# A ready time moved back by one microsecond in the list schedule of the second mixer's unit matmuls

## The chip, the cores and the metric

The kernel runs on one core of one Trainium2 chip. The metric is the device time of one execution in microseconds, as the median of the runs of a kernel. The profile and its trace come from one further execution on the same core.

## The reference, cut to what matters

Two decoder layers on 256 tokens of width 2048, all in float32. The first layer mixes tokens with RWKV-7, the second with a chunked gated DeltaNet; behind each comes a gated MLP with a short convolution, and behind every part a layer norm. The change lies in the second mixer:

```python
def gated_deltanet(x, w_in, conv_w, a_log, dt_bias, norm_w, w_out):
    proj = x @ w_in
    qkv, z, b, a = jnp.split(proj, ...)
    qkv = silu(causal_dwconv(qkv, conv_w))
    q, k, v = ...                              # 16 key heads, 32 value heads of 128
    o = chunk_gated_delta_rule(q, k, v, g, beta)
    o = o * rsqrt(mean(o * o) + NORM_EPS) * norm_w * silu(z)
    return o.reshape(B, T, GDN_VALUE_DIM) @ w_out
```

The delta rule solves a unit lower triangular system in each chunk and head (`Tm = triangular_solve(A + eye, eye)`), and carries a state from one chunk to the next.

## The kernel before, in words

Products of float32 numbers are made from two parts of each operand, a rounded one (`whi`, `xhl`) and the rest (`wlo`), three matmuls for a product. The weights stream from memory: a tile `raw` is loaded, ScalarE casts it to `whi`, VectorE subtracts to get `wlo`, TensorE multiplies. These projections are the *main* stream. In the second mixer they are written (`gdn`, L1531) as eight rounds, u = 0 to 7; each round projects the q, k, v and z of four value heads (576 matmuls of 128x256 named `mm<-xhl,whi` and `mm<-xhl,wlo`). Behind the eighth round comes the output projection, whose matmuls are named `tm<-whi,ohl`.

After each round `gdn_unit` (L1645) records a *unit*, the delta rule of those four heads, as a side stream. A unit is one long chain that goes to and fro between the engines. The names that the text uses, in order of the chain: `vT` and `kqT` (transposes), `sq`, `ssq`, `rn`, `nk` (norms), `kk` (products of keys), `lt` and `at` (masked with decays `gr`), then the inverse (`inverse`, L917): `uc`, `z`, `spread`, the matmul `blocks`, fourteen small VectorE steps `t` and `v`, `vx`, the matmul `zp<-vx`, `n<-x,ld`, three matmul groups `y`, `zp<-y`, `xt`, `xb` (two of them), two groups `n<-xb`, six groups `y`; then for each of two chunks the solve (`u<-rhr,y`, `au`, `du`, `un`), `S`, `ks`, `qs`, `os`, `o`, `ms` and the transpose `oT`, whose result `og` the output projection reads.

Nothing is issued in the order in which it is written. Every operation is first recorded, and a list scheduler (`order`, L364) replays the whole program against estimated durations (`cost`) and hand-over times (`LAT`, `LAT_TO`) and writes out one order for each engine; each engine then runs its list in that order. All instructions carry line 556, the line that issues them, so names and not lines tell them apart. At most two units (`DEPTH_G = 2`) are open at a time. Some steps (`nc.two`, `nc.copy`) have a form for two engines, and the scheduler picks one: `spread`, `xb`, `uc<-uc` and `o<-o,os` on VectorE or GpSimd.

At each step the scheduler takes the operation with the smallest key. For a unit's matmul the key began with `s`, the later of the time at which TensorE is free and the time at which the operands are estimated to be there; a main matmul with the same time comes behind it. So a unit's matmul was put in front of the main ones at the very moment at which its operands were estimated to be ready.

Of the kernel before, what the change touches and what calls it, by code (L numbers as in the profile page):

```python
# [28 lines left out]
NU = 8  # L29
# [52 lines left out]
class Buf:  # L82


    def __init__(self, pool, shape, dtype, tag, bufs, name, real=None):
        self.pool, self.shape, self.dtype, self.name, self.real = pool, list(shape), dtype, name, real
        self.group = None if pool is None else pool.group(tag or name, bufs)
        self.tag = tag or name
        self.writers, self.readers, self.uses = [], [], 0
        self.pe = self.read = None  # L90
        self.end = 0.0
# [60 lines left out]
class View:  # L152
# [5 lines left out]
    def then(self, shape, dtype, *op):  # L158
        return View(self.buf, shape, dtype, self.ops + (op,))
# [72 lines left out]


class Op:
    __slots__ = ("lazy", "eng", "calls", "dur", "preds", "succ", "soft", "at", "bufs", "news", "stream", "idx", "npred", "ready",
                 "out", "fn", "alts", "least", "held", "evac", "table")


# [13 lines left out]
class Plan:  # L252
# [2 lines left out]


    def __init__(self, tc):
        self.lazy = 0.0
        self.tc, self.real = tc, tc.nc
        self.main = Stream(False, 0)  # L260
        self.streams, self.cur = [self.main], self.main
        self.last_pool = None
        self.tensor, self.vector, self.scalar, self.gpsimd, self.sync = (
            Engine(self, n) for n in ("tensor", "vector", "scalar", "gpsimd", "sync"))
# [9 lines left out]
    def op(self, eng, stream):  # L274
        o = Op()
        o.eng, o.calls, o.dur, o.preds, o.succ, o.soft, o.bufs, o.news = eng, [], 0.0, set(), [], [], set(), []
        o.stream, o.idx, o.ready, o.out, o.fn, o.alts = stream, len(stream.ops), 0.0, None, None, None
        o.npred, o.held, o.evac, o.lazy, o.table = 0, 0.0, [], self.lazy, None
        stream.ops.append(o)
        return o  # L280

# [18 lines left out]
    def two(self, out, x, y, op):  # L300
        self.either(*((e, "tensor_tensor", (out, x, y, op), {}) for e in ("vector", "gpsimd")))
# [62 lines left out]
    def order(self):  # L364
# [51 lines left out]
        while len(done) < total:  # L416
            best = None
            for e in engines:
                f = free[e]
                for o in cand[e]:  # L420
                    r = o.ready
                    ok = True
                    for b in o.news:
                        g = b.group
                        if g["free"] is None:
                            g["free"] = [0.0] * g["bufs"]
                        if (len(g["free"]) < len(o.news) or g["queue"][o.stream][0] not in o.news
                                or not self.spare(g, o, active)):
                            ok = False
                            break  # L430
                        r = max(r, g["free"][0])
                    if not ok:
                        continue
                    for b in o.evac:

                        if b.read is not None and b.read[0] != e:
                            r = max(r, b.read[1] + LAT[b.read[0]] + LAT_TO[e])
                    s = max(f, r)
                    if o.alts:
                        s += o.alts[e][3] - o.least  # L440
                    elif e == "scalar" and o.table not in (None, table):
                        s += TABLE
                    if e != "tensor":
                        key = (s, 0, o.ready - AGE_V * o.stream.age, o.idx)
                    else:
                        key = ((s, 0, o.ready - AGE * o.stream.age, o.idx) if o.stream.side
                               else (s + o.lazy, 1, o.idx, 0))
                    if best is None or key < best[0]:
                        best = (key, o, e, max(f, r))
# [5 lines left out]
            _, o, e, s = best  # L455
# [8 lines left out]
            dur = o.dur  # L464
# [3 lines left out]
            if e == "tensor":  # L468
                while (win + 1) * HAM <= s:
                    u = busy.get(win, 0.0) / HAM  # L470
# [133 lines left out]
KEEP = True  # L604
AGE, AGE_V, AGE_M = 1e5, 1e5, -9
HAM, HAM_ON, HAM_OFF = 4096 / 1.2, 0.7, 0.375
LAZY = 200.0

TABLE, TABLES = 1283.0, {AF.Tanh: 0, AF.Exp: 0, AF.Square: 0, AF.Silu: 1, AF.Ln: 2}
GROUP = 700.0  # L610
# [7 lines left out]
class Trunk:  # L618
# [468 lines left out]
    def rwkv(self):  # L1087
# [127 lines left out]
        wo = a["rw_w_o"]  # L1215
        nc.lazy = LAZY
        for c0, n in (0, 1024), (1024, 512):
# [313 lines left out]
    def gdn(self):  # L1531
        nc, a = self.nc, self.a
# [59 lines left out]
        def qkv(ps, b, nme, u, j, gblk):  # L1592
            d = st.setdefault(u, {})
            if nme == "q" and b == 0:
                d["KQ"] = self.ws.tile([P, 2, 2, 2, P], F32, tag="KQ", bufs=2, name="KQ")
            if nme == "v" and j == 0 and b == 0:
                d["v"] = self.ws.tile([P, 4, T], F32, tag="v_u", name="v_u")
            acc = self.conv(ps, gblk + b, 4, 64)
            if nme == "v":
                silu2(d["v"][:, 2 * j + b, :], acc)  # L1600
            else:
                silu2(d["KQ"][:, b, :, int(nme == "q"), :], acc)

        def zev(ps, b, u, j):
            d = st[u]
            if j == 0 and b == 0:
                d["z"] = self.ws.tile([P, 4, T], F32, tag="z_u", bufs=2, name="z_u")
            silu2(d["z"][:, 2 * j + b, :], ps)

        for u in range(NU):  # L1610
            self.proj_fm(w, u * 256, 256, xk, lambda ps, b, u=u: qkv(ps, b, "q", u, 0, 2 * u))
            if u == 0:
                self.proj_fm(w, 12288, 64, xk, gates)
            self.proj_fm(w, D + u * 256, 256, xk, lambda ps, b, u=u: qkv(ps, b, "k", u, 0, 16 + 2 * u))
            for j in range(2):
                self.proj_fm(w, 2 * D + u * 512 + j * 256, 256, xk,
                             lambda ps, b, u=u, j=j: qkv(ps, b, "v", u, j, 32 + 4 * u + 2 * j))
            for j in range(2):
                self.proj_fm(w, 4 * D + u * 512 + j * 256, 256, xk,
                             lambda ps, b, u=u, j=j: zev(ps, b, u, j))  # L1620
            with nc.unit(DEPTH_G):
                self.gdn_unit(u, st[u])

        self.ok = {}
        wo = a["gdn_w_out"]
# [249 lines left out]
```

## Time and profile before

| | |
|---|---|
| median of 3 runs | 3112.74 us (3106.1 to 3119.25) |
| the profiled execution | 3101.99 us, of which its span is 3100.3 us |
| TensorE busy | 2992.3 us, 97% of the span |
| VectorE busy | 2110.6 us, 68% |
| ScalarE busy | 1615.9 us, 52% |
| GpSimd busy | 651.7 us, 21% |
| granted TensorE clock, mean | 0.988 of 2.4 GHz |

Times in the trace count from the start of the span. The second mixer's projections run from 1420 us to 2158 us. The first unit's inverse begins at 1518 us, and a new unit follows every 90 us or so. TensorE is busy in nearly all of the span, so time is lost where it idles or where its clock is lowered.

### The profile page before, as it was taken

Reading aid. Unit: us, or ns where it says so; the run is one execution under the profiler, and the core shown is the slowest. Engines: PE = TensorE matmul, PEld = TensorE weight load, DVE = VectorE, ACT = ScalarE, POOL = GpSimd, SP = SyncE. Lnnn points to the kernel's source line nnn. Section 1 sums busy time; section 2 is a strip of 40 time slices with the busy share of each in tenths; the row PEclk is TensorE's granted clock in tenths of the full one; section 3 lists DMA queues with packets and bytes.
Section 4 is the critical chain, followed back from the end, with each engine's and each line's share of the span. In section 5 each row is a group of like instructions: output and inputs, shape, how many; then the busy total and the mean of one; then the engine's idle time right before and its main releaser. Section 6 shows DMA issues by size and latency. Waiting matters only on the chain.

```text
span 3100.3 us, 55990 instructions
## 1 busy us (share of the span) xinstructions
PE 2992.3 (97%) x22307; PEld 2797.3 (90%) x22307; DVE 2110.6 (68%) x3316; ACT 1615.9 (52%) x2713; POOL 651.7 (21%) x569
## 2 busy tenths in 40 slices
PE   8998999899999999998999999999999999999998
PEld 7998898779999998887999999999788999999886
DVE  7657878767666665447777777787767666666445
ACT  4437666445555554345556555555566555555333
POOL 3014344325010110003322112111233410101001
PEclk9999999999999999999999999999999999999999
DMA  6652213246666665665555554554465666666655
GB/s 198 206 165 89 74 58 97 68 132 199 189 184 188 186 184 190 193 192 155 169 151 150 143 144 137 143 155 131 152 192 182 201 188 185 188 186 186 192 189 187
DMA packets 436119, 503.64 MB, mean 162 GB/s; under 512 B 22769, under 2 KB 367121, under 8 KB 435857
## 3 DMA queue, kind: packets, MB, share of 16 engines
q1 hardware_dynamic: 435856, 500.06, 53.9%
q8 instruction: 175, 2.87, 0.4%
q14 instruction: 88, 0.71, 0.1%
HBM read 497.87 MB, written 2.13 MB: 161 GB/s over the span
## 4 chain that ended last, share of the span: by engine, by line
PE 79%; DVE 11%; issue 4%; POOL 2%; DMA 2%; ACT 2%; SPq 0%; DVEq 0%; POOLq 0%; ACTq 0%
PE mm L556 49%; PE tm L556 22%; DVE wlo L556 3%; PE y L556 1%; PE au L556 1%; DMA gr<-gdram 1%; PE gm L556 1%; PE n L556 1%; PE kv L556 1%; ACT whi L556 1%; DVE y L556 1%; DVE uc L556 1%; DMA og<-in_ln_ffn_g 1%; PE o L556 0%; DVE v L556 0%
## 5 line engine op out<-in xcount | busy, mean ns | idle before, releaser
L556 DVE TENSOR_TENSOR wlo<-raw,whi 128x1024 fp32r<-128x1024 f32 (+1 forms) x898 | 1110.1, 1237 | 651.4 <-ACT whi L556 649.7
L556 PE MATMUL mm<-xhl,whi 128*128 128x256 f32 x8584 | 1535.8, 283 | 4.4 <-POOL xhl L556 2.2
L556 ACT CAST whi<-raw 128x1024 fp32r<-128x1024 f32 (+2 forms) x917 | 941.0, 1027 | 816.3 <-PE mm L556 476.5
L556 PEld LDWEIGHTS mm<-xhl,whi 128*128 128x128 f32 x8584 | 1322.2, 191 | 8.4 <-POOL xhl L556 3.3
L556 PE MATMUL mm<-xhl,wlo 128*128 128x256 f32 (+1 forms) x4376 | 1215.4, 283 | 3.6 <-DVE wlo L556 3.4
L556 PEld LDWEIGHTS mm<-xhl,wlo 128*128 128x128 f32 x4376 | 819.6, 189 | 5.7 <-DVE wlo L556 3.8
L556 PE MATMUL tm<-whi,hhl 128*128 128x512 f32 x1312 | 407.6, 391 | 0.0
L556 DVE SCALAR_TENSOR_TENSOR acc<-mm,taps,acc 128x255 f32<-128x255 f32 (+2 forms) x522 | 248.5, 479 | 93.1 <-ACT acc L556 85.5
L556 PEld LDWEIGHTS tm<-whi,hhl 128*128 128x128 f32 x1312 | 246.4, 188 | 52.0
L556 PE MATMUL mm<-mixhl,whi 128*128 128x256 f32 x1536 | 278.1, 283 | 12.8 <-ACT mixhl L556 7.7
L556 POOL TENSOR_TENSOR hhl<-acc,hhl 128x256 fp32r<-128x256 f32 x84 | 101.3, 1206 | 758.0 <-ACT hhl L556 758.0
L556 PE MATMUL tm<-wlo,hhl 128*128 128x512 f32 x656 | 257.3, 392 | 0.4 <-DVE wlo L556 0.3
L556 PEld LDWEIGHTS mm<-mixhl,whi 128*128 128x128 f32 x1536 | 237.9, 192 | 15.6 <-ACT mixhl L556 7.7
L556 PE MATMUL mm<-mixhl,wlo 128*128 128x256 f32 x768 | 219.4, 291 | 4.8 <-DVE wlo L556 4.0
L556 ACT ACTIVATE acc<-mm,taps 128x256 f32<-128x256 f32 x230 | 124.2, 541 | 152.9 <-PE mm L556 152.6
L556 PE MATMUL tm<-whi,ohl 128*128 128x512 f32 x480 | 156.7, 399 | 1.9 <-DVE z_u L556 1.9
L556 PEld LDWEIGHTS mm<-mixhl,wlo 128*128 128x128 f32 x768 | 146.0, 192 | 8.8 <-DVE wlo L556 5.0
L556 PEld LDWEIGHTS tm<-wlo,hhl 128*128 128x128 f32 x656 | 123.1, 188 | 29.8 <-DVE wlo L556 1.1
L556 POOL TENSOR_TENSOR wlo<-raw,whi 128x1024 fp32r<-128x1024 f32 (+2 forms) x19 | 44.1, 2324 | 435.5 <-ACT whi L556 431.5
L556 PEld LDWEIGHTS tm<-whi,ohl 128*128 128x128 f32 x480 | 91.0, 189 | 21.4 <-DVE z_u L556 2.3
L556 POOL TENSOR_TENSOR ms<-ms,mhalf 128x4 f32<-128x4 f32 (+1 forms) x24 | 32.4, 1350 | 366.0 <-DVE ms L556 364.5
L556 PE MATMUL tm<-wlo,ohl 128*128 128x512 f32 x240 | 94.1, 392 | 0.0
(324 smaller groups left out, 3319.9 us busy)
## 6 DMA issues: line engine op xcount, KB each, us to landing
raw<-in_ffn_w_up SPq DMA_DIRECT2D x336, 512.0 KB, 3.8
raw<-in_gdn_w_in SPq DMA_DIRECT2D x192, 512.0 KB, 3.8
raw<-in_ffn_w_down SPq DMA_DIRECT2D x168, 512.0 KB, 4.3
raw<-in_gdn_w_out SPq DMA_DIRECT2D x64, 512.0 KB, 4.3
raw<-in_rw_w_v SPq DMA_DIRECT2D x32, 512.0 KB, 4.3
raw<-in_rw_w_r SPq DMA_DIRECT2D x32, 512.0 KB, 3.6
raw<-in_rw_w_o SPq DMA_DIRECT2D x32, 512.0 KB, 3.7
raw<-in_rw_w_k SPq DMA_DIRECT2D x31, 512.0 KB, 4.4
```

The costliest lines, as they stand in the source:

```text
L556: i = getattr(getattr(self.real, o.eng), fn)(*(val(a) for a in args), **{k: val(a) for k, a in kw.items()})
```

## The change

Operations of TensorE in a side stream get a number `slack`. In the second mixer it is 1000 ns for units 0 to 6 and 0 for unit 7; the first mixer's units keep 0. The key of a unit's matmul now begins with the later of the free time and the ready time plus the slack. Only the choice is moved: where the matmul is chosen, its estimated start is still the later of the free time and the ready time.

```diff
         o.npred, o.held, o.evac, o.lazy, o.table = 0, 0.0, [], self.lazy, None
+        o.slack = self.slack if eng == "tensor" and stream.side else 0.0
...
-                        key = ((s, 0, o.ready - AGE * o.stream.age, o.idx) if o.stream.side
+
+                        key = ((max(f, r + o.slack), 0, o.ready - AGE * o.stream.age, o.idx) if o.stream.side
                                else (s + o.lazy, 1, o.idx, 0))
...
-LAZY = 200.0
+LAZY, SLACK = 200.0, 1000.0
...
             with nc.unit(DEPTH_G):
+                nc.slack = SLACK if u < NU - 1 else 0.0
                 self.gdn_unit(u, st[u])
+                nc.slack = 0.0
```

The main matmuls keep their order among themselves, and no instruction is added or taken away. Outside the second mixer TensorE's order is the same row for row.

The first place is the middle of unit 4's inverse on TensorE, from the matmul `zp<-y` to the solve. In the kernel before, with 15, 15, 6, 6, 6 and 9 main matmuls where the dots stand:

```order
L556 MATMUL zp<-y,perms 128x256
...
L556 MATMUL n<-xb,ltr 128x96 x4
...
L556 MATMUL n<-xb,ltr 128x96 x4
L556 MATMUL y<-y,n 32x32 x4
...
L556 MATMUL y<-y,n 32x32 x4
...
L556 MATMUL y<-y,n 64x64 x8
...
L556 MATMUL y<-y,n 32x96 x8
...
L556 MATMUL u_22491<-rhr,y 128x128 x4
```

In the changed kernel, with 30, 21, 18, 15, 18 and 3 main matmuls where the dots stand:

```order
L558 MATMUL zp<-y,perms 128x256
...
L558 MATMUL n<-xb,ltr 128x96 x4
...
L558 MATMUL n<-xb,ltr 128x96 x4
L558 MATMUL y<-y,n 32x32 x4
...
L558 MATMUL y<-y,n 32x32 x4
L558 MATMUL y<-y,n 64x64 x4
...
L558 MATMUL y<-y,n 64x64 x4
L558 MATMUL y<-y,n 32x96 x4
...
L558 MATMUL y<-y,n 32x96 x4
...
L558 MATMUL u_22695<-rhr,y 128x128 x4
```

Between two steps of the chain stand two to three times as many main matmuls as before; from `zp<-y` to `u` they are 57 before and 105 now.

The second place is TensorE ahead of unit 4's matmul `blocks`. In the kernel before, with 24, 6 and 114 main matmuls where the dots stand:

```order
L556 MATMUL kqT<-cst,KQ 128x128 x4
...
L556 MATMUL oT<-cst,o 128x128 x4
...
L556 MATMUL kk<-KQ 128x256 x4
...
L556 MATMUL blocks<-spread,perms 128x512
```

In the changed kernel, the last piece of the same stretch, with 6 and 60 main matmuls where the dots stand:

```order
L558 MATMUL kk<-KQ 128x256
L558 MATMUL qs<-S_21589,KQ 128x256
L558 MATMUL o<-un,at 128x128 x3
L558 MATMUL kk<-KQ 128x256
...
L558 MATMUL o<-un,at 128x128
...
L558 MATMUL blocks<-spread,perms 128x512
```

Unit 3, whose chain is longer now, is not done when unit 4 begins: its solve, `qs` and `o` of the second chunk stand among the `kk` of unit 4, where before only its `oT` was left. Between `kqT` and `blocks` the main matmuls are 144 before and 132 now.

The third place is GpSimd's list in the same stretch, from unit 4's `rn` on. Before:

```order
L556 TENSOR_TENSOR rn<-ssq,mhalf 128x8
L556 AFFINE_SELECT gr<-gr 128x512 x2
L556 AFFINE_SELECT lt<-lt 128x512 x2
L556 TENSOR_TENSOR ld<-lt,cst 128x4x4x32 x2
L556 TENSOR_TENSOR y<-z_22373,cst 128x512 x2
```

In the changed kernel:

```order
L558 TENSOR_TENSOR rn<-ssq,mhalf 128x8
L558 AFFINE_SELECT lt<-lt 128x512 x2
L558 TENSOR_TENSOR o<-o,os 128x512
L558 TENSOR_TENSOR uc<-uc,cst 128x256
L558 TENSOR_TENSOR spread<-z_22044,cst 128x512
L558 TENSOR_TENSOR ms<-ms,mhalf 128x4
L558 TENSOR_TENSOR ld<-lt,cst 128x4x4x32
L558 AFFINE_SELECT gr<-gr 128x512 x2
L558 TENSOR_TENSOR xb<-xt,cst 128x384
L558 TENSOR_TENSOR y<-z_22508,cst 128x512
L558 TENSOR_TENSOR xb<-xt,cst 128x384
```

`o<-o,os` of unit 3, and `uc<-uc`, `spread` and both `xb` of unit 4, have moved from VectorE to GpSimd.

## Rows read from the trace of the kernel before

**Rows 1.** The head of the profile's page.
```profile
span 3100.3 us, 55990 instructions
```

**Rows 2.** Windows: the second mixer from unit 0's inverse on, and its passage to the output projection.
```profile
core 0: us, PE busy (x) PEld busy (x) DVE busy (x) ACT busy (x) POOL busy (x), PEclk, DMA share, GB/s
1510.00:2150.00 640.00, 614.07 (x5265) 602.04 (x5264) 493.14 (x942) 359.55 (x684) 116.91 (x83) 0.97 0.51 144
2150.00:2200.00 50.00, 45.34 (x264) 37.36 (x263) 43.71 (x86) 26.96 (x55) 18.74 (x14) 0.97 0.43 142
```

**Rows 3.** Waits of TensorE, 1510 to 2150 us: total, times, longest.
```profile
PE blocks L556 <- DVE spread L556: 13.0, 6, 3.6
PE n L556 <- DVE xb L556: 7.5, 5, 1.5
PE zp L556 <- DVE vx L556: 3.3, 5, 1.3
PE blocks L556 <- POOL spread L556: 1.1, 1, 1.1
PE n L556 <- POOL xb L556: 1.0, 2, 0.5
```

**Rows 4.** Timeline of TensorE: three waits (in brackets), of units 0, 1 and 4.
```profile
1522.34 0.80 PE L556 MATMUL blocks<-spread,perms 128*128 128x512 f32 x1 [3.57 <-DVE spread L556]
...
1634.88 0.65 PE L556 MATMUL n<-xb,ltr 128*128 128x96 f32 x4 [0.50 <-POOL xb L556]
...
1908.36 0.62 PE L556 MATMUL n<-xb,ltr 128*128 128x96 f32 x4 [1.47 <-DVE xb L556]
```

**Rows 5.** Windows of 10 and 20 us with their clocks; columns as in rows 2.
```profile
1520.00:1530.00 10.00, 7.66 (x44) 7.57 (x45) 7.87 (x23) 2.97 (x4) 0.25 (x1) 0.66 0.53 153
1630.00:1640.00 10.00, 9.40 (x96) 8.81 (x95) 9.20 (x13) 6.17 (x13) 6.68 (x4) 1.00 0.37 108
1710.00:1720.00 10.00, 8.69 (x71) 8.24 (x70) 8.69 (x22) 4.37 (x8) 0.00 (x0) 0.83 0.54 156
1810.00:1830.00 20.00, 18.52 (x161) 17.96 (x162) 12.98 (x19) 10.40 (x21) 3.52 (x2) 0.91 0.38 107
1880.00:1890.00 10.00, 8.12 (x56) 7.88 (x56) 8.87 (x19) 4.90 (x9) 4.62 (x3) 0.83 0.64 182
1910.00:1920.00 10.00, 10.00 (x74) 9.73 (x73) 2.43 (x4) 3.84 (x10) 0.00 (x0) 0.66 0.38 106
2000.00:2010.00 10.00, 9.55 (x71) 9.25 (x72) 3.11 (x4) 4.01 (x9) 0.00 (x0) 0.66 0.24 71
2090.00:2100.00 10.00, 8.52 (x76) 7.96 (x76) 4.83 (x5) 5.41 (x11) 2.38 (x2) 0.83 0.37 107
```

**Rows 6.** Groups by operation, VectorE and GpSimd, 1510 to 2150 us: busy us, mean ns.
```profile
L556 DVE TENSOR_TENSOR xb<-xt,cst 128x384 fp32r<-128x384 f32 x11 | 11.5, 1049 | 0.1
L556 DVE TENSOR_TENSOR o<-o,qe 128x512 f32<-128x512 f32 x14 | 9.6, 686 | 7.6 <-PE o L556 7.6
L556 DVE TENSOR_REDUCE z<-uc 128x64 f32<-128x256 f32 x7 | 4.2, 598 | 0.7 <-POOL uc L556 0.6
L556 POOL TENSOR_TENSOR xb<-xt,cst 128x384 fp32r<-128x384 f32 x3 | 4.1, 1356 | 30.8 <-ACT th L556 16.2 <-DVE xt L556 14.6
L556 POOL TENSOR_TENSOR spread<-z,cst 128x512 fp32r<-128x512 f32 x1 | 2.0, 2012 | 3.3 <-DVE v L556 3.3
L556 POOL TENSOR_TENSOR uc<-uc,cst 128x256 f32<-128x256 f32 x1 | 1.8, 1772 | 1.3 <-DVE uc L556 1.3
```

**Rows 7.** The chain that ended last, in unit 0: sixty main matmuls on end.
```profile
1560.49 7.07 PE mm L556 x60
```

**Rows 8.** Timeline of GpSimd and VectorE in unit 7.
```profile
2164.86 0.64 POOL L556 TENSOR_SCALAR_AFFINE_SELECT lt<-lt 128x512 f32<-128x512 f32 x1 [5.17 <-DVE lt L556]
...
2167.27 0.43 DVE L556 TENSOR_TENSOR ohl<-og,ohl 128x256 fp32r<-128x256 f32 x1 [2.48 <-ACT ohl L556]
2167.61 0.57 DVE L556 COPY uc<-lt 32x256 f32<-32x256 f32 x2
```

More of the change, by code (lines that the diff above doesn't have):

```diff
@@ L234 @@
 class Op:
-    __slots__ = ("lazy", "eng", "calls", "dur", "preds", "succ", "soft", "at", "bufs", "news", "stream", "idx", "npred", "ready",
+    __slots__ = ("slack", "lazy", "eng", "calls", "dur", "preds", "succ", "soft", "at", "bufs", "news", "stream", "idx", "npred", "ready",
                  "out", "fn", "alts", "least", "held", "evac", "table")
@@ L257, in __init__ @@
     def __init__(self, tc):
-        self.lazy = 0.0
+        self.lazy = self.slack = 0.0
         self.tc, self.real = tc, tc.nc
```

## The prediction

> **What bounds the kernel now.** I read the windows by stage first. TensorE is the engine that sets the time, so the only question for a stage is where it idles and at what clock it works. From unit 0's inverse to the eighth round, 640 us, it is busy for 614.07 us: 25.9 us are idle, at a mean clock of 0.97 [rows 2]. VectorE is busy for 493.14 us of it, 77%, so it has room on the whole. The list of TensorE's waits then says that the 25.9 us are three places and no others [rows 3]: `blocks` waits for `spread` (13.0 + 1.1 us, once in each of units 0 to 6), `n` waits for `xb` (7.5 us in five units, 1.0 in two), and `zp` waits for `vx` (3.3 us in five units). In each the waiting matmul belongs to a unit, and behind it in TensorE's list stand main matmuls that could have run. The reader should see in these rows what kind of mistake it is: the operand comes later than the list assumed, by 0.5 to 3.6 us, always at the same steps.
>
> The clock is the second half of the loss. Seven windows show where it falls to its lower level, 1.2 of 2.4 GHz [rows 5]. A window of 10 us at 0.66 has lost 3.4 us of work, one at 0.83 has lost 1.7, and 20 us at 0.91 have lost 1.8. The seven together: 3.4 + 1.7 + 1.8 + 1.7 + 3.4 + 3.4 + 1.7 = 17.1 us. Each lies just behind one of the waits: the first behind the wait of 3.57 us, the window at 1910 us behind one of 1.47 us [rows 4, 5]. Behind the wait of 0.50 us in unit 1 the clock stayed at 1.00 [rows 4, 5].
>
> So the stage holds 25.9 + 17.1 = 43 us that a better place for these matmuls could give back, 1.4% of the span [rows 1].
>
> **The change, part by part.** Nothing is added or removed; the matmuls of units 0 to 6 are moved back in TensorE's list. A step is taken 1.0 us after the estimated ready time instead of at it, and main matmuls fill that microsecond. A step whose operand comes w us late then waits for about w - 1.0.
>
> *blocks.* Seven waits, all above 1.0, sum 14.1: what is left is 14.1 - 7 x 1.0 = 7.1 us. I check this by one chain in the changed order. In unit 4, from the last `o` of unit 3 to `blocks` stand 60 main matmuls, 7.07 us [rows 7]. The work that `blocks` now waits for in that time is `o<-o,qe` on VectorE, 0.69, `o<-o,os` on GpSimd, for which the nearest row is GpSimd's `spread` of the same size, 2.01, then `uc`, 1.77, the reduction `z`, 0.60, and `spread`, 2.01: 7.1 us [rows 6], and some 0.1 us (an estimate) for each of five hand-overs. The wait is about 0.5 us, where the subtraction leaves 0.9 of a mean wait of (13.0 - 3.6) / 5 = 1.9 us [rows 3]. I keep the 7.1. The bounds are 2.6 (only unit 0's 3.57 - 1.0 is left) and the 14.1 of now.
>
> *zp.* The longest of the five waits is 1.3 us, so at most 0.3 us is left of each that exceeds 1.0; of 3.3 us I leave 0.3.
>
> *n.* The five waits for VectorE's `xb` sum to 7.5 and leave 2.5; the two for GpSimd's `xb`, 0.5 each, leave nothing [rows 3]. `xb` moves to GpSimd in most units, where it takes 1.36 us instead of 1.05 [rows 6], but the two `n` of unit 4 now have 51 main matmuls ahead of them from `zp<-y` on instead of 30. Bounds: 0 to 8.5.
>
> Left over: 7.1 + 0.3 + 2.5 = 9.9; given back: 25.9 - 9.9 = **16.0 us**, between 0 and 23.
>
> *Clock.* Four of the seven windows (1810, 1910, 2000 and 2090 us) follow the wait for VectorE's `xb`, some 1.5 us each; they hold 1.8 + 3.4 + 3.4 + 1.7 = 10.3 us. With 0.5 us left of these waits I take them as given back, because the 0.50 us of unit 1 at the same place cost no clock. The small `y` matmuls that follow also stand among two to three times as much main work as before. Of the others I count the window at 1710 us (behind waits of 1.1 and 1.3 us) and that at 1880 us (behind unit 4's `blocks`) as given back, 3.4 us, and unit 0's as staying, since 2.6 us of its wait stay. Given back: **13.7 us**, between 0 and 17.1. This is the weaker of the two terms: the waits of some 1.9 us at `blocks` in units 3, 5 and 6 were followed by no fall, none of their windows is among the seven, so length alone does not settle it.
>
> *What the units' longer way costs.* Each unit now ends later by 15 to 25 us of main matmuls, in the next unit's first part. For units 0 to 5 that lies beside other work. Unit 6's second chunk now falls where the output projection begins, and there VectorE is the busy engine: 43.71 of 50 us, with TensorE idle for 4.7 us [rows 2]. About eight operations of unit 6, 0.69 us each by the row of `o<-o,qe` [rows 6], come into that stretch: 5.5 us. VectorE has 6.3 us free there, but in pieces. I take a loss of **2 us**, between 0 and 5.5. Unit 7 has no slack, so its own waits in that window stay.
>
> *The queue on VectorE.* With unit 3's tail among unit 4's `lt` and `at`, VectorE's list holds `un`, `os` and `o`, which wait for TensorE, ahead of work for `spread`. In unit 7 the trace shows what this can do: GpSimd finished `lt` at 2165.5 us, yet VectorE's `uc<-lt` began at 2167.61, behind an `ohl` that waited 2.48 us for ScalarE [rows 8]. The Trainium skill (TensorE: Matmul & The Clock Gate, section "Architectural detail: the array is 16× 32×32, not 1× 128×128") says that VectorE and ScalarE serve their queues strictly first in, first out, and this row agrees. By that rule the four operations of a tail that come late would push `spread` back by their whole time, and the sum would be the third rival's below; by the chain above, which already has `o` in it, they fit in the time that TensorE gives them. I hold to the chain.
>
> Sum against the profiled execution: 3101.99 - 16.0 - 13.7 + 2 = 3074.3 us. The timed runs lie higher, at a median of 3112.74 us; the same 27.7 us off it gives **3085 us**, 0.9% faster.
>
> **The rivals.** *First: the waits shrink and the clock does not come back.* The falls could belong to the stretches of small matmuls and not to the waits before them; those three waits without a fall speak for it, the quiet unit 1 speaks against it. Then 16.0 - 2 = 14 us are gained: 3099 us.
>
> *Second: the waits form again at their old size.* The scheduler plans the whole mixer anew with the same wrong estimates, and puts `uc`, `spread` and `o<-o,os` on GpSimd, where `uc` and `spread` take 1.77 and 2.01 us [rows 6]; and it brings `blocks` forward against `kqT`, 132 main matmuls instead of 144. If that eats the microsecond, nothing is gained and up to 5.5 us are lost in the passage: 3107 to 3118 us. That the change does nothing it says is excluded by its order of instructions: the steps of the inverse are two to three times as far apart.
>
> *Third, slower: VectorE's queue.* If the previous unit's tail stands in front of `spread` and comes late, each of units 1 to 6 waits longer at `blocks`. Now it is (14.1 - 3.6) / 6 = 1.75 us; with four operations in front, 2.7 us, less the slack, it would be 1.75 + 2.7 - 1.0 = 3.5 us, six times 20.7. With 2.6 of unit 0, 0.3 and 2.5, idle time would be 26.1 us, as now. A wait of that length was followed by 3.4 us of lost clock in unit 0, so seven of them cost 23.8 instead of 17.1, and the passage 5.5: 12 us slower, 3125. With all eight operations in front it is 29 us slower, 3142. It decides from about 2 us of backlog in each unit on. Against it: VectorE's 77%.
>
> **How the numbers follow.** Chances: the forecast 0.68, the first rival 0.13, the second 0.11, the third 0.08. If everything came back, 43 us, the time would be 3070. The forecast's own range is 3070 to 3097. The range of 8 in 10 reaches from 3068 to 3108: it takes in the first rival and the better half of the second, and leaves out the third. A change of about 0.5%, 15.6 us, is what a measurement of this kernel can tell from none. Faster by more than that: nearly all of the forecast and some of the first rival, 0.72. Within it: the rest of the first, most of the second and a little of the third, 0.22. Slower: 0.06.
>
> **What would show it.** Right: in TensorE's waits of units 0 to 6 `zp` and `n` are nearly gone and `blocks` has about 7 us; the windows behind `n` in units 3 to 6 have a clock of 1.00; the stage is about 30 us shorter. Unit 7 still waits at `blocks` and `zp`. Wrong: `blocks` at 10 us or more, or low clock behind waits under a microsecond (first rival); waits for `wlo` in the main matmuls, or VectorE idle at `un` or `o` while `spread` is due (third); more than 5 us of new idle time at the beginning of the output projection.

## The result, and the profile after

| | before | after |
|---|---|---|
| median, runs of one chip | 3110.88 us (3106.1 to 3119.25, 4 runs) | 3065.36 us (3062.13 to 3070.28, 4 runs) |
| ratio | | 0.9859, 95% interval 0.9831 to 0.9886 |
| profiled execution | 3101.99 us | 3062.13 us |

The changed kernel is 45.5 us faster. The forecast was 3085 with a range from 3068 to 3108: the sign and the main mechanism are as predicted, the gain is larger than forecast, and the time lies 3 us below the range.

The head of the page of the changed kernel and its line of busy times:

```profile
span 3060.4 us, 55981 instructions
...
PE 2978.3 (97%) x22307; PEld 2787.5 (91%) x22307; DVE 2099.5 (69%) x3291; ACT 1617.1 (53%) x2729; POOL 659.0 (22%) x578
```

The windows that answer to [rows 2], columns as there. The eighth round now ends 37.5 us earlier in the trace (the first `tm` of the output projection starts at 2120.6 instead of 2158.1 us), so the stage is cut at 2110 and the passage at 2160 us:

```profile
1510.00:2110.00 600.00, 594.43 (x5235) 586.04 (x5235) 483.42 (x913) 356.13 (x687) 127.21 (x94) 1.00 0.55 153
2110.00:2160.00 50.00, 48.43 (x302) 40.66 (x301) 45.61 (x95) 32.95 (x70) 16.65 (x13) 1.00 0.45 147
```

TensorE idles for 5.57 us of the stage instead of 25.93 [rows 2], and its clock is 1.00 in all of it: none of the seven low windows of [rows 5] has a counterpart. In the passage it idles for 1.57 us instead of 4.66, at 1.00 instead of 0.97.

TensorE's waits in the same stage (us in total, times, longest), which answer to [rows 3]:

```profile
PE zp L558 <- DVE vx L558: 4.0, 4, 1.5
PE blocks L558 <- POOL spread L558: 1.5, 3, 0.6
```

`n`, 8.5 us before, no longer waits at all. `blocks` has gone from 14.1 to 1.5 us; `zp` has not shrunk (3.3 before, 4.0 now). Three rows of TensorE's timeline: `blocks` of unit 0, which waited 3.57 us [rows 4], and `blocks` and `zp` of unit 4, whose `blocks` the prediction followed by hand:

```profile
1522.46 0.50 PE L558 MATMUL blocks<-spread,perms 128*128 128x512 f32 x1 [0.36 <-POOL spread L558]
...
1866.43 0.49 PE L558 MATMUL blocks<-spread,perms 128*128 128x512 f32 x1 [0.59 <-POOL spread L558]
...
1876.73 0.35 PE L558 MATMUL zp<-vx,perms 128*128 128x256 f32 x1 [0.73 <-DVE vx L558]
```

The waits of the passage, where unit 7 without slack follows. Before (2110 to 2200 us):

```profile
PE tm L556 <- DVE z_u L556: 1.9, 1, 1.9
PE blocks L556 <- DVE spread L556: 1.4, 1, 1.4
PE zp L556 <- DVE vx L556: 1.3, 1, 1.3
```

After (2110 to 2165 us):

```profile
PE blocks L558 <- POOL spread L558: 0.9, 1, 0.9
PE zp L558 <- DVE vx L558: 0.5, 1, 0.5
PE tm L558 <- DVE z_u L558: 0.3, 1, 0.3
```

**A measure that leaves the first mixer out.** A whole execution also holds the first mixer, whose loss varies from run to run (below). What the change alone does is read from two marks on TensorE: the first `kqT`, at the start of unit 0, and the last `lnT`, the transposes of the layer norm behind the output projection. I call the time between them *the stretch*. The two marks by tile, before (the last numbers are the first and the last start):

```profile
L556 PE MATMUL kqT<-cst,KQ x24: 272/272/273, 1503.1 to 1686.5; 128*128 128x128 f32 x24
...
L556 PE MATMUL lnT<-cst,res x32: 270/273/328, 2351.3 to 2365.9; 128*128 128x128 f32 x32
```

and after:

```profile
L558 PE MATMUL kqT<-cst,KQ x24: 272/273/273, 1505.6 to 1675.0; 128*128 128x128 f32 x24
...
L558 PE MATMUL lnT<-cst,res x32: 272/273/329, 2311.4 to 2326.0; 128*128 128x128 f32 x32
```

The stretch is 2365.9 - 1503.1 = 862.8 us before and 2326.0 - 1505.6 = 820.4 us after: 42.4 us. The windows give the same sum by cause: 20.4 of waits in the stage, 17.1 of clock there [rows 5], 3.1 of waits in the passage and 50 x 0.03 = 1.5 of clock there, 42.1 us in all.

### The profile page after: what moved, and what is told of

Its sections match the earlier page's. It is cut to its first block, busy times and chain, and to the rows that moved or that the text cites. A ratio compares the mean times of both kernels' runs of the same rounds, so it can differ in the third digit from the quotient of the medians.

```text
span 3060.4 us, 55981 instructions
## 1 busy us (share of the span) xinstructions
PE 2978.3 (97%) x22307; PEld 2787.5 (91%) x22307; DVE 2099.5 (69%) x3291; ACT 1617.1 (53%) x2729; POOL 659.0 (22%) x578
## 4 chain that ended last, share of the span: by engine, by line
PE 85%; DVE 9%; issue 2%; POOL 2%; ACT 1%; DMA 1%; SPq 0%; DVEq 0%; POOLq 0%; ACTq 0%
PE mm L558 53%; PE tm L558 23%; DVE wlo L558 2%; PE y L558 1%; PE au L558 1%; PE n L558 1%; PE gm L558 1%; PE kv L558 1%; ACT whi L558 1%; DVE v L558 0%; DVE t L558 0%; PE vT L558 0%; PE o L558 0%; DVE uc L558 0%; PE du L558 0%
## 5 line engine op out<-in xcount | busy, mean ns | idle before, releaser
L558 DVE SCALAR_TENSOR_TENSOR acc<-mm,taps,acc 128x255 f32<-128x255 f32 (+1 forms) x522 | 249.3, 479 | 85.6 <-ACT acc L558 77.3
L558 PEld LDWEIGHTS mm<-mixhl,whi 128*128 128x128 f32 x1536 | 237.4, 192 | 17.1 <-ACT mixhl L558 8.0
```

Of the source, the lines that this page charges most:

```text
L558: i = getattr(getattr(self.real, o.eng), fn)(*(val(a) for a in args), **{k: val(a) for k, a in kw.items()})
```

## The experiments

Each run changes the kernel after, if nothing else is said. The stretch, the idle time and the clock are those of the profiled execution; the idle time is that from 1510 to 2110 us (not read for the run whose second mixer begins 130 us later). Clock lost is the sum over windows of 10 us in the same stage. Medians are of timed runs beside the kernel before on the same chip, which had 3110.15, 3108.74 and 3107.36 us in the three sets.

| run | median, us (range) | ratio, 95% | stretch | idle | clock lost |
|---|---|---|---|---|---|
| before | 3110.88 | 1 | 862.8 | 25.9 (to 2150) | 17.0 |
| after | 3065.36 (3062 to 3070) | 0.983 to 0.989 | 820.4 | 5.6 | 0 |
| slack at three steps only | 3083.45 (3077 to 3088) | 0.984 to 0.994 | 836.7 | 13.1 | 0 |
| slack at all other steps | 3093.4 (3083 to 3106) | 0.991 to 0.996 | 844.6 | 24.4 | 3.4 |
| slack 500 | 3094.74 (3089 to 3111) | 0.992 to 0.997 | 847.1 | 18.2 | 10.2 |
| slack 2000 | 3067.98 (3060 to 3076) | 0.979 to 0.989 | 816.2 | 1.0 | 0 |
| unit 6 without slack | 3070.94 (3068 to 3072) | 0.984 to 0.991 | 828.5 | 7.3 | 0 |
| unit 7 with slack | 3070.51 (3065 to 3086) | 0.984 to 0.995 | 824.9 | 6.5 | 0 |
| first mixer with slack | 3201.16 (3197 to 3204) | 1.026 to 1.034 | 821.0 | | |
| measured durations, no slack | 3081.25 (3072 to 3091) | 0.988 to 0.994 | 836.8 | 12.8 | 6.8 |
| measured durations and slack | 3061.15 (3057 to 3072) | 0.983 to 0.988 | 813.5 | 0.4 | 0 |
| 2000, unit 6 1000, unit 7 none | 3062.04 (3061 to 3063) | 0.983 to 0.987 | 814.4 | 1.1 | 0 |
| the change again | 3067.47 (3062 to 3070) | 0.985 to 0.989 | 821.1 | 6.2 | 0 |
| slack on the first mixer's `blocks` too | 3080.1 (3072 to 3086) | 0.988 to 0.993 | 821.4 | 6.4 | 0 |

### The two halves: the steps that wait, and all the others

The slack is set only around the three matmuls that the prediction costed (`blocks`, `zp<-vx`, `n<-xb`), and in the second run around all others of the unit and not these:

```diff
+        nc.slack = nc.base        # and 0 in the second run
         self.mm(ps, perm(2), spread.rearrange("p k s t -> p (k s t)"))
+        nc.slack = 0.0            # and nc.base in the second run
```

> The slack stands on three matmuls of each unit alone: blocks, zp<-vx and the two n<-xb, the ones that waited. All other steps of the chain are taken at their estimated ready time, so the small y matmuls stand as close as in the kernel before. Theory A (the waits themselves bring the clock down): TensorE's idle time from 1510 us to the end of the stage is 5 to 10 us, the clock is 1.00 in all its windows of 10 us, and the time is within 8 us of the change (3057 to 3073). Theory B (the clock falls because the small matmuls stand close): the idle time goes as under A, but the windows behind n keep a clock of 0.66 to 0.93, some 10 us of lost work, and the time is 3072 to 3085. For the passage to the output projection: if the longer units made it shorter, it is back at 4.7 us of idle time here, since these units are longer by four steps and not by some thirty.

> The opposite: slack on every unit matmul except blocks, zp<-vx and n<-xb, which are taken at their estimated ready time as in the kernel before. The small y matmuls are spread out. Theory A: the waits at the three steps come back, 20 to 26 us, the clock falls behind them as before (12 to 17 us of work), and the time is 3095 to 3110. Theory B: the waits come back but the clock stays at 1.00 behind n, and the time is 3080 to 3092. If the waits do not come back either, the estimates were not what made the operands late, and another part of the new order did.

Neither run came out as one of the theories had it. The first has theory A's clock (nothing lost) but, at 3083 us, theory B's time; the second is, at 3093 us, just above theory B's range and still loses 3.4 us of clock.

With slack at the three steps only, the waits and the window of the stage:

```profile
PE blocks L558 <- DVE spread L558: 7.2, 5, 2.6
PE n L558 <- DVE x L558: 2.4, 5, 0.5
PE zp L558 <- DVE vx L558: 1.8, 2, 0.9
...
PE blocks L558 <- POOL spread L558: 0.2, 1, 0.2
...
1510.00:2110.00 600.00, 586.88 (x5149) 575.01 (x5148) 485.10 (x930) 344.25 (x653) 114.96 (x83) 1.00 0.53 150
```

With slack at all steps but these:

```profile
PE zp L558 <- DVE vx L558: 8.7, 7, 1.9
PE blocks L558 <- POOL spread L558: 6.0, 4, 1.6
PE n L558 <- DVE xb L558: 5.5, 3, 1.8
PE blocks L558 <- DVE spread L558: 2.8, 3, 1.6
...
1510.00:2110.00 600.00, 575.56 (x5026) 564.73 (x5025) 462.20 (x877) 345.35 (x664) 115.21 (x87) 0.99 0.53 149
```

The first half is the prediction's own subtraction, and it holds there: `blocks` keeps 7.4 us, where w - 1.0 had said 7.1. The second half shows what the subtraction left out: slack that is *not* at `blocks` takes 14.1 - 8.8 = 5.3 us off its wait. Two things change with it, and this run does not part them: the steps ahead of `blocks` are moved back as well, and the list, planned anew, gives steps of the chain to other engines (in units 2 to 6 ScalarE has all four of the copies `uc<-lt`, of which it had two or three before; why that matters stands at the durations below). The two add: 14.1 - 6.7 - 5.3 = 2.1, and the change has 1.5. The wait at `zp`, which has no slack here, grows from 3.3 to 8.7 us. On the stretch the halves nearly add too: 26.1 us are gained by the one, 18.2 by the other, and 42.4 by both.

The clock came back in both, almost whole: 0 and 3.4 us are lost, where the kernel before loses 17. In the first half the `y` matmuls stand as close as before, and the clock never falls. So close small matmuls alone do not bring it down in this stage. The second half shows less than it seems to. As much is idle as before (24.4 us), but not in the same places: the longest wait at `blocks` is 1.6 us instead of 3.6, and three waits at `n` exceed a microsecond instead of five. The clock falls behind two of these three, by 1.7 us each, although the `y` matmuls behind them now stand among main work:

```profile
1746.19 0.62 PE L558 MATMUL n<-xb,ltr 128*128 128x96 f32 x4 [1.83 <-DVE xb L558]
...
1926.29 0.62 PE L558 MATMUL n<-xb,ltr 128*128 128x96 f32 x4 [1.83 <-DVE xb L558]
```

In the three traces of the kernel before (two of them below) 11 of 15 waits of some 1.5 us at `n` have a fall behind them, of 1.7 or 3.4 us. So the falls of this stage stand behind waits, and they went with the long waits at `blocks` and most of those at `n`; that the close `y` matmuls have a part in it is not shown.

### Half and double the slack

```diff
-LAZY, SLACK = 200.0, 1000.0
+LAZY, SLACK = 200.0, 500.0       # and 2000.0
```

> A slack of 500 ns in place of 1000. By the subtraction that the prediction used (a wait of w leaves w minus the slack), the waits of the kernel before leave 14.1 - 3.5 = 10.6 us at blocks, about 1.7 at zp and 5.0 at n, 17 us in all, and with waits of about 1 us behind n some of the falls of the clock stay: 3080 to 3095. If each replanned order makes its own waits, the idle time differs from this sum by more than 5 us, as it did at 1000 ns step by step (zp 4.0 for 0.3, blocks 1.5 for 7.1, n 0 for 2.5).

> A slack of 2000 ns. By the subtraction the stage's idle time goes from 5.6 us to under 2 us (what is left is one wait of the first unit, 1.6 us), a gain of up to 4 us against 1000 ns: 3058 to 3066. Rival: units that are longer by another thirty microseconds come into each other's way and into the output projection, and the passage loses 3 us or more: 3066 to 3080.

With 500 ns, 15.7 of the stretch's 42.4 us are gained, and 10.2 us of clock are lost. 18.2 us stay idle, close to what the subtraction gives in sum (14.1 - 7 x 0.5 at `blocks`, 7.5 - 5 x 0.5 at `n`, 1 at `zp`: 16.6), but not where it has them: `zp` has 12.2 us and `blocks` 2.7. With 2000 ns the stage is all but free of waits (1.0 us), yet the time from the first `tm` to the last `lnT` grows from 205.4 to 212.0 us: the passage takes back 6.6 of the 10.8 us that the way up to it gives. The stretch is 4.2 us shorter, and the medians do not differ.

### The last two units

```diff
-                nc.slack = SLACK if u < NU - 1 else 0.0
+                nc.slack = SLACK if u < NU - 2 else 0.0     # and SLACK for all
```

> The slack stands on units 0 to 5 only; unit 6 is placed as in the kernel before. It isolates the passage to the output projection. If unit 6's later end is what made the passage shorter (TensorE idle 4.7 us before, 1.6 with the change, and its low clock gone), the passage is back at 4 to 5 us of idle time, and unit 6's own waits and low clock come back too, 4 to 6 us: 3070 to 3080. If the later end costs time, as the prediction had it, the passage is shorter than with the change and the time is 3060 to 3068.

> The slack stands on all eight units. Unit 7's waits (blocks 0.9 and zp 0.5 us with the change) go, and its last step comes later against the output projection's matmuls by some 9 us. If the projection's first blocks cover that, the time is that of the change within 4 us: 3061 to 3069. Rival: the projection waits for unit 7's result, and the time rises by up to those 9 us: 3069 to 3078.

The prediction feared that unit 6's later end would cost at the output projection. Taking the slack off it makes the stretch 8 us longer, not shorter. A wait of that run's passage, and one of the run with slack on unit 7 as well:

```profile
PE zp L558 <- POOL vx L558: 2.3, 1, 2.3
```

```profile
PE tm L558 <- ACT ohl L558: 3.0, 1, 3.0
```

The first wait is one of unit 7 and not of unit 6: without slack unit 6 itself waits for 1.46 us at `zp` and 0.48 at `n`, 0.8 us more than with it (0.59 at `blocks`, 0.53 at `zp`). The loss is in the passage, 2110 to 2160 us, where TensorE idles for 4.3 us at a clock of 0.93 instead of 1.6 at 1.00. Unit 7 with slack is late itself: its last `oT` starts at 2217.0 instead of 2201.1 us, the output projection waits 3.0 us for its `ohl`, and the stretch is 4.5 us longer. In the timed runs neither differs from the change by more than their ranges.

### Better durations in place of slack, and with it

The waits say that the list expects the operands too early. Here its estimates for some of the costliest operations of units 0 to 6 are set near the means of the trace, once with slack 0 and once with 1000:

```diff
+        if eng == "gpsimd":
+            if len(args) > 3 and args[3] == ALU.pow:
+                return 300.0 * n
+            return 3.0 * n + 270 if fn == "tensor_tensor" else 706.0
+        if eng == "vector":
+            if name == "xb":
+                return 1049.0
+            if fn == "tensor_reduce" and n == 64:
+                return 598.0
...
```

> No slack. Instead the estimates of the unit's operations, in units 0 to 6 of the second mixer, are set to what the trace of the kernel before shows: GpSimd's powers 300 ns an element, its two-operand operations 3.0 ns an element and 270, the triangular masks 706, VectorE's xb 1049, the reduction z 598, and 65 ns more for each of the small steps t and v. If the waits come from estimates that are too short, most of the 25.9 us go without any slack (left: under 10 us) and the time is 3070 to 3090. If they come from VectorE running late as a whole, behind the main stream's subtractions, the waits stay at 15 us or more and the time is 3095 to 3112.

> The changed kernel, and for units 0 to 6 also the durations that the trace shows (the list of the run before that had these alone). Costs alone left 12.8 us of idle time in the stage and 6.8 us of lost clock; the slack alone left 5.6 and 0. If the two halves add, the microsecond covers nearly every step that is still late: at most 3 us idle, clock 1.00, a profile some 3 to 4 us below that of the change, median 3056 to 3066. Rival: the lateness that is left comes from queues that no duration describes, and it stays; then as the change, 3062 to 3070, with 5 us idle in the stage.

The durations alone take the idle time from 25.9 to 12.8 us, nearly all that is left at `blocks` (10.6 us, longest 3.9). So the durations set right are about half of the lateness. For much of the rest the traces show a duration that is not one number. The copies `uc<-lt` at the head of the inverse take 0.28 us each on VectorE while GpSimd is idle [rows 8], and mostly 1.25 to 1.37 us while GpSimd runs `ld`. Unit 3 in the kernel before, and in the run with measured durations (three copies, the first two slow):

```profile
1790.55 4.02 POOL L556 TENSOR_TENSOR ld<-lt,cst 128x512 fp32r<-128x512 f32 x2
1790.62 1.36 DVE L556 COPY uc<-lt 32x256 f32<-32x256 f32 x1 [0.74 <-POOL lt L556]
...
1783.75 2.58 POOL L558 TENSOR_TENSOR ld<-lt,cst 128x512 fp32r<-128x512 f32 x2
1783.81 2.97 DVE L558 COPY uc<-lt 32x256 f32<-32x256 f32 x3 [0.33 <-POOL lt L558]
```

Before, the units with such copies are 0, 3, 4, 5 and 6, the five that wait for 1.9 to 3.6 us at `blocks`. In the run with measured durations units 0, 3 and 5 have two or three slow copies, and they are its three waits of over 2 us (3.88, 2.49 and 2.40). The list has one estimate for this copy, and this run did not change it. With the slack of the change only two of these copies are slow (1.15 us), since the new plan gives ScalarE 21 of the 28 instead of 16: a part of what `blocks` gained is this, by luck. That GpSimd causes the slowness is not shown by itself; no run moves `ld` alone.

With the slack on top the stage's waits and window are:

```profile
PE blocks L558 <- DVE spread L558: 0.3, 1, 0.3
...
1510.00:2110.00 600.00, 599.58 (x5291) 592.03 (x5290) 487.54 (x939) 363.46 (x699) 126.89 (x96) 1.00 0.56 155
```

TensorE is busy for 599.58 of 600 us: what the durations leave, the microsecond covers, but for 0.3 us.

### A slack that ends in steps, and the change again

```diff
-                nc.slack = SLACK if u < NU - 1 else 0.0
+                nc.slack = (2 * SLACK if u < NU - 2 else SLACK) if u < NU - 1 else 0.0
```

> Slack 2000 for units 0 to 5, 1000 for unit 6, 0 for unit 7. By the trace of slack 2000 on all seven the stage should have 1 us idle, 4 less than the change, and by that of the change the passage to the output projection should take 205.4 us again instead of 212.0: a profile of 3058, a median 4 us below the change's, 3061. Rival: what the passage lost there came from units 4 and 5 being late, not from unit 6 alone; then the passage takes 209 to 212 us again and the time is that of the change, 3063 to 3068.

> The changed kernel as it is, beside the other three on this chip, to see what a repeat is worth: 3062 to 3070, and a clock of 0.991 over the timed runs. If the low clock of the kernel before were a matter of the run and not of its order, the clock would here fall to 0.984 in some run, and the time reach 3080.

The graded slack has the stage of slack 2000 (1.1 us idle) and the passage of the change (205.0 us); its stretch is 814.4 us, 6 us below the change's two traces (820.4 and 821.1). The timed runs agree in size, 3062.04 against 3067.47 us beside each other, but their ranges and the ratios' intervals overlap. Both this and the run with measured durations beat the change by the trace, by 6 to 8 us or 0.2%.

### The first mixer

The first run sets the slack on all matmuls of the first mixer's units 0 to 6 too, the second only on their `blocks`:

```diff
+                    nc.slack = SLACK if v < NU - 1 else 0.0   # second run: nc.base, used at blocks
                     self.rwkv_unit(v, d, kr)
+                    nc.slack = 0.0
```

> The same slack on the units 0 to 6 of the first mixer as well, on top of the change. TensorE idles for 50 us in the first 700 us, at a clock of 0.97 to 0.99. If those waits are of the same kind, an operand estimated some hundred ns too early with main matmuls behind it, half of them go: 3025 to 3050. Rival: the first mixer's idle time comes from VectorE (84 to 87% busy between 300 and 600 us) or from a chain whose end the next projection needs, four units being open at a time; then longer units gain nothing or lose: 3060 to 3085.

> The changed kernel, with the slack also on the matmul blocks, and on no other, of units 0 to 6 of the first mixer. Theory (slack pays at a step that waits and costs at one that does not, where VectorE or the chain of a unit sets the pace): of the 8.3 us that blocks waits for spread there in four units, 4 go, no other step is moved back, and the time is 3061. Rival (every microsecond put into a chain of the first mixer is one of the mixer's end, since its units and not its projections set the pace there): seven microseconds are added, the clock falls as it did with slack on all steps, and the time is 3072 to 3100.

Slack on everything makes the kernel 3% slower than before, which neither expectation had. Its window over the first mixer, whose clock is 0.76 where the kernel before has 0.99 (its row stands below):

```profile
300.00:750.00 450.00, 411.53 (x2562) 353.21 (x2560) 270.57 (x551) 211.86 (x489) 123.24 (x154) 0.76 0.17 53
```

Its first `kqT` of the second mixer starts at 1639.8 us, some 130 us later than in the other traces; by windows of 10 us it loses 130 us to the clock in the first 900 us, where the change's two traces lose 19 and 22, and idles for 67 us instead of 50. With slack on `blocks` alone, the waits did what my theory said. The wait at `blocks` in the first 1000 us, in the change's second trace:

```profile
PE blocks L558 <- DVE spread L558: 8.2, 4, 2.5
```

and in this run:

```profile
PE blocks L558 <- DVE spread L558: 1.4, 2, 1.2
```

The time did not follow. The median is 12.6 us above the change's, and all six runs (3071.5 to 3086.3 us) lie above all five of the change beside them. Their granted clock is lower as well, 0.983 to 0.988 over the whole run where those five have 0.989 to 0.994. In the trace the second mixer starts at 1528.6 instead of 1510.7 us; windows of this run:

```profile
300.00:750.00 450.00, 428.77 (x3141) 379.62 (x3142) 338.57 (x674) 253.74 (x556) 168.92 (x184) 0.91 0.28 86
...
600.00:630.00 30.00, 30.00 (x148) 24.91 (x147) 14.55 (x37) 10.37 (x24) 9.85 (x11) 0.50 0.11 36
```

From 600 to 630 us TensorE has no idle time at all and runs at 1.2 GHz throughout. What it did as the clock fell, by its timeline:

```profile
592.49 0.40 PE L558 MATMUL tm<-whi,yhl 128*128 128x512 f32 x1
...
593.69 0.88 PE L558 MATMUL kv<-vt,ka 128*128 128x64 f32 x6 [0.28 <-POOL ka L558]
594.40 0.61 PE L558 MATMUL kv<-vt,kr 128*128 128x64 f32 x4
594.82 1.18 PE L558 MATMUL n<-x,ld 128*128 128x24 f32 x8
...
598.98 0.63 PE L558 MATMUL tm<-whi,yhl 128*128 128x512 f32 x1
```

The same `tm` takes 0.40 us ahead of these small matmuls and 0.63 behind them, and the longest wait between is 0.28 us; the last longer one, 1.67 us, ended at 584.43 us. So this fall stands behind small matmuls and not right behind a wait.

But such a stretch needs no slack in the first mixer. The run with slack 500 has none there, and TensorE's order is that of the change up to the second mixer. Its trace:

```profile
390.00:430.00 40.00, 40.00 (x224) 37.25 (x223) 14.28 (x29) 16.41 (x41) 9.29 (x15) 0.50 0.12 36
300.00:750.00 450.00, 419.96 (x3153) 373.57 (x3153) 340.35 (x682) 252.82 (x557) 163.00 (x181) 0.94 0.28 87
```

It is at 1.2 GHz for 40 us without idling, and its second mixer starts at 1527.6 us, as late as with slack on `blocks`. So the timed runs show that the slack on `blocks` costs time at a lower clock, and this one trace does not show which stretch the slack has brought. Nor does the clock account for all of it: the first 900 us lose 41 us to it instead of 22 and idle for 40 instead of 50, 9 of the 18 us by which the second mixer starts later. Why the clock stays low without a wait, and why the slack lowers it in this mixer and not in the second, no run tells.

### The kernel before, traced again

11 us were open: the gap between the profiled execution of before and its timed runs. The kernel before was run unchanged.

> The kernel before, traced a second time. If the difference between its profile (3102) and its timed runs (3108 to 3113) is clock lost in the second mixer, which the change takes away, the windows from 1510 to 2150 us lose more than the 17 us of the first trace in a run near the median. If it is clock lost in the first mixer, which neither kernel is rid of, those windows lose 17 us again and the windows from 300 to 700 us lose some 10 more than in the first trace.

> The kernel before, traced a third time, with the same two readings as the second: over 17 us of lost clock from 1510 to 2150 us, or some 10 us more than in the first trace from 300 to 700 us.

The windows of the first trace of before, in the first mixer:

```profile
300.00:750.00 450.00, 418.86 (x3306) 373.55 (x3305) 356.47 (x695) 261.80 (x567) 177.68 (x186) 0.99 0.31 97
```

of the second trace, with the second mixer's stage:

```profile
300.00:750.00 450.00, 420.98 (x3289) 375.19 (x3288) 352.04 (x693) 260.37 (x570) 178.01 (x187) 0.97 0.31 95
1510.00:2150.00 640.00, 612.94 (x5269) 601.51 (x5268) 493.14 (x937) 359.70 (x685) 115.47 (x83) 0.98 0.51 145
```

and of the third:

```profile
300.00:750.00 450.00, 420.97 (x3261) 375.94 (x3261) 350.45 (x690) 258.60 (x563) 175.46 (x184) 0.97 0.31 95
1510.00:2150.00 640.00, 614.14 (x5252) 602.88 (x5251) 491.29 (x936) 358.73 (x685) 115.33 (x83) 0.97 0.51 144
```

The stage repeats: 27.1 and 25.9 us idle, 0.98 and 0.97, with its low windows at partly other places. The first mixer does not: by windows of 10 us, 300 to 750 us lose 5.1 us of clock in the first trace, 11.9 and 15.3 in the others, and 11.9 in the changed kernel's. The stretch of the second trace is 2372.3 - 1510.3 = 862.0 us, that of the third 863.8, beside 862.8 of the first. So the 7 us by which these two executions (3108.62 and 3108.69 us) are longer than the first trace lie ahead of the stretch, where the change has no part; of the executions above 3109 us no trace was taken. The unchanged kernel's 10 timed runs (3103.9 to 3126.55, median 3112.86) came out at a ratio of 1.0026 to before's own 13, with an interval from 1.0006 to 1.0047 that should hold 1: on this kernel, ratios within some 0.5% say little.

## Why the prediction was right in kind and too small

Three terms of the sum failed: the waits were forecast to give back 16.0 us and gave 20.4, the clock 13.7 and gave 17.1, and the passage was to cost 2 and gave 4.6. The first two had their size wrong, the third its sign.

- **The three waits as the loss, given back by main work:** right. `n` and `blocks` went as main matmuls filled in. (The main matmuls between the steps of unit 4's inverse are 105 instead of 57, 1.8 times as many, and not two to three times as the prediction has it.)
- **`blocks`, 7.1 us left:** mis-sized, 1.5 measured. The subtraction counts only the step's own microsecond. That part is right (7.4 with slack at the three steps alone). Left out were the 5.3 us that the slack of the other steps takes: the subtraction holds each operand's lateness fixed, and the new plan changed it, down to which copies run beside GpSimd's `ld`. The chain by hand for unit 4 said 0.5 us and 0.59 was measured; I had it beside the subtraction's 0.9 and kept the subtraction.
- **`zp`, 0.3 left; `n`, 2.5 left:** wrong in opposite ways, and by luck near in sum (2.8 and 4.0). `zp` kept 4.0, perhaps since what is late ahead of `blocks` shows up there; `n` kept nothing. The waits together gave back 20.4 us, not 16.0.
- **Clock, 13.7:** the right place, mis-sized; 17.1 came back. Unit 0's 3.4 were to stay because 2.6 us of its wait would; the wait fell to 0.4 us. The reason given (waits at `n`) fits: with slack at the three steps alone the waits for `xb` go and nothing is lost. The thinner `y` matmuls, named beside it, are not shown to matter.
- **Passage, a loss of 2:** the wrong sign. Unit 6's eight operations on VectorE did not delay the projection; unit 7's waits and the one of `tm` for `z_u` shrank, 4.6 us gained with the clock. Without slack on unit 6 the stretch is 8 us longer.
- **The sum:** 27.7 forecast, 42.1 measured on the stretch: 4.4 from the waits, 3.4 from the clock, 6.6 from the passage. It is the case called "everything came back", which stood at the edge of the forecast's own range.
- **The base:** 3112.74 less 42.1 is 3070.6. The other 5 us lie outside the stretch. Most likely they are the base, a median of three runs: further sets of before have medians of 3107 to 3113, and single runs scatter by 20 us and more.
- **The first rival** (the clock belongs to stretches of small matmuls) is wrong for this stage; in the first mixer one fall was seen with no wait over 0.3 us in the 11 us ahead of it. **The second** (waits form again) is seen in one small part, `zp`. **The third** did not come: VectorE is busy for 483.42 of 600 us, 81%, and no wait for `wlo` is in the stage's list; so the tail of four operations fitted in. The sentence that the Trainium skill (TensorE: Matmul & The Clock Gate, section "Architectural detail: the array is 16× 32×32, not 1× 128×128") has on queues served first in, first out is not contradicted, but the backlog that it would have needed was not there.

## What to carry to other kernels

Where the engine that sets the time waits for side work that a plan thinks is ready, one margin on all of the side work's steps can be worth more than one on the steps that are seen to wait, here 42 us against 26: the plan changes with it, and with the plan the lateness. Try it stage by stage: the same microsecond cost 3% in the first mixer, mostly through the clock, and some microseconds in the last unit, behind which nothing was left. Before setting one duration for an operation, see whether it has only one: the copy `uc<-lt` has two. Compare traces between two marks that enclose the change; here that repeats within 2 us, where whole runs scatter by 20.

## What was not expected of the hardware

- TensorE's clock can fall, and stay at 1.2 GHz for 30 us, while TensorE has no idle time at all (600 to 630 us in the run with slack on the first mixer's `blocks`; 390 to 430 us in the run with slack 500). The Trainium skill (TensorE: Matmul & The Clock Gate, section "HAM oscillation — how this bites in real kernels") puts such falls down to waits between groups of matmuls; the second mixer's falls, each behind a wait of over a microsecond, agree in kind, and these long stretches without a wait do not.
- The same order of the first mixer loses 5.1 to 26.5 us to the clock from 300 to 750 us (5.1 in the first trace of before, 26.5 in that of slack 500), while the second mixer of one kernel repeats within 2 us.
- VectorE's copy `uc<-lt` of 32x256 takes 0.28 us while GpSimd is idle and 0.74 to 1.37 us, once 2.47, beside GpSimd's long two-operand operations.
